# Attention with a fixed order on TensorE: a step's value products in pieces behind the next step's scores

## The chip, the cores and the metric

The kernel runs on one core of one Trainium2 chip. A time is device microseconds (us) of one execution; of several, the median is taken. The engines of the core are TensorE (PE; its weight loads are a row of their own, PEld), VectorE (DVE), ScalarE (ACT), GpSimd (POOL) and SyncE (SP), whose queue issues most of the DMAs. Each engine works through its own list of instructions in the order in which they stand there and waits on semaphores for the others.

## The reference

Two transformer blocks over 1024 tokens of width 1024. Two of its layers hold an attention over eight heads of width 64, and these are all that the change touches:

```
s = (einsum('bqhd,bkhd->bhqk', q_nope, k_nope) + einsum('bqhr,bkr->bhqk', q_rope, k_rope)) * scale
s = where(causal, s, -inf);  p = softmax(s);  o = einsum('bhqk,bkhd->bqhd', p, v)      # first layer
...
s = where(valid, q.k * HEAD_DIM**-0.5 - slope * distance, -inf)                        # mixing layer,
p = exp(s - max); o = p.v / sum(p); the branches are merged by their denominators      # three dilations
```

The kernel computes the three dilated branches as one causal attention with a table added to the scores, so both layers use one function. All matmuls are in 32-bit floats; products that need the precision are taken as a high and a low part.

## The kernel before, in words

The kernel is written against a layer that traces all instructions first and then fixes each engine's list with a scheduler: an instruction may stand anywhere that its data, the buffers of its pools and explicit edges allow. `turn(K, trace)` traces a piece of work so that its TensorE instructions stand behind the last TensorE instruction traced so far; in the attention of the kernel before nothing is held by it.

`attention` (L359) does one head. It takes the queries in four steps j = 0..3 of two blocks of 128 (u = 0, 1). In a step, for each block, the scores against keys 0..kend (kend = 128, 256, ... 1024) go to a bank of PSUM, in three matmul passes in the first layer and two in the mixing layer (L381). VectorE adds the mask or table and takes the row minimum (L385), ScalarE takes the exponential and the row sum (L387). Then, for each pair of key blocks, a *chunk*: three or four transposes (L394) turn the probabilities, ScalarE copies them from PSUM as the high part (`split`, L140), VectorE subtracts to get the low part (L141), and four products with the values (L400: high and low for each of two key blocks) add to the step's output. A step has j + 1 chunks. It closes with a copy on ScalarE (L403) and an add on VectorE (L404); after steps 1 and 3 the reciprocal sums are transposed (L410) and multiplied in (L412).

Around each head stands one `step(hd)` of the output projection (`early`, L725; matmuls L695): 12 matmuls of 512 columns in the first layer, 24 in the mixing layer, with rows of the layer's other half (`s`, loaded by SP at L708 and split on ScalarE and VectorE at L140 and L141). Its result is added to the residual on VectorE (L594) in the first layer and copied by ScalarE (L1793) in the mixing layer. SP also loads the query and key rows of a coming head (L608 and L610: eight DMAs in the first layer; L1810: six in the mixing layer) into one of two tiles, once the last scores of the head two before it have been read; behind them in SP's queue comes the load of `s`.

In the two attentions the scheduler interleaves scores, transposes, products and the projection of neighbouring steps and heads, and lets the products lag behind the scores. Pools: two PSUM tiles for scores and projection (`pa`), four for transposes and outputs (`pb`).

Of the kernel before, what the change touches and what calls it, by code (L numbers as in the profile page):

```python
# [14 lines left out]
AF = mybir.ActivationFunctionType  # L15
ALU = mybir.AluOpType
AX = mybir.AxisListType

P = 128
# [31 lines left out]
def _pools(ctx, tc):  # L51
    K = Ctx()
    K.tc = tc
    K.nc = tc.nc
    E = mybir.EngineType
    K.pe, K.sp, K.act, K.dve, K.pool = E.PE, E.SP, E.Activation, E.DVE, E.Pool
    mk = lambda n, b, **kw: ctx.enter_context(tc.tile_pool(name=n, bufs=b, **kw))
    K.cp = mk("cst", 1)
    K.px = mk("px", 4)
    K.pp = mk("pp", 4)  # L60
    K.pq = mk("pq", 4)
    K.pr = mk("pr", 2)
    K.ps = mk("ps", 2)
    K.pl = mk("pl", 3)
    K.pwst = mk("pwst", 2)
    K.pwh = mk("pwh", 4)
    K.pwl = mk("pwl", 4)
    K.pj = mk("pj", 1)
    K.pt = mk("pt", 2)
    K.pA = mk("psA", 2, space=bass.MemoryType.PSUM)  # L70
    K.pB = mk("psB", 4, space=bass.MemoryType.PSUM)
    K.pd = mk("dr", 1, space=bass.MemoryType.DRAM)
    K.n = 0
    K.last = None

    def nm(p):
        K.n += 1
        return f"{p}{K.n}"

    K.nm = nm  # L80
    K.X = lambda dt=F32R: K.px.tile([P, 4, 1024], dt, tag="x", name=nm("x"))
    K.P2 = lambda dt=F32: K.pp.tile([P, 2, 1024], dt, tag="p", name=nm("p"))
    K.Q2 = lambda dt=F32: K.pq.tile([P, 2, 1024], dt, tag="q", name=nm("q"))
    K.R2 = lambda dt=F32: K.pr.tile([P, 2, 1024], dt, tag="r", name=nm("r"))
    K.S = lambda dt=F32: K.ps.tile([P, 1024], dt, tag="s", name=nm("s"))
    K.L = lambda dt=F32: K.pl.tile([P, 1024], dt, tag="l", name=nm("l"))
    K.A = lambda: K.pA.tile([P, 1024], F32, tag="a", name=nm("pa"))
    K.B = lambda: K.pB.tile([P, 512], F32, tag="b", name=nm("pb"))
    K.junk = lambda: K.pj.tile([P, 512], mybir.dt.bfloat16, tag="j", name=nm("j"))
    K.DR = lambda shape, dt=F32: K.pd.tile(shape, dt, tag=nm("dt"), name=nm("d"))  # L90

    def small(cols, tag, dt=F32, bufs=2):
        return K.pt.tile([P, cols], dt, tag=tag, name=nm(tag), bufs=bufs)

    K.small = small
    return K
# [41 lines left out]
def split(K, hi, lo, src, eng=None):  # L138

    K.nc.scalar.activation(hi, src, AF.Copy)  # L140
    (eng or K.nc.vector).tensor_tensor(lo, src, hi.bitcast(F32), ALU.subtract)  # L141
# [26 lines left out]
def turn(K, trace):  # L168

    with K.tc.issue_after(anchor(K)):  # L170
        trace()
# [184 lines left out]
        nc.vector.scalar_tensor_tensor(out[:, s:], raw[:, :T - s], w(3 - s), out[:, s:], ALU.mult, ALU.add)  # L356


def attention(K, qb_passes, table, scale, vt, out, p0, ring, chunks):  # L359

    nc = K.nc
    st = K.small(24, "ast", bufs=3)
    low, tot, rec = (st[:, 8 * n:8 * n + 8] for n in range(3))
    for j in range(4):
        n = 2 * j + 2
        sm = []
        a = None  # L370
        for u in range(2):
            qb = 2 * j + u
            kend = (qb + 1) * P
            if j > 1 or u == 0:
                a = K.A()
            av = a if j > 1 else a[:, 512 * u:512 * u + 512]
            ps = qb_passes(qb)
            for h in range(0, kend, 512):
                e = min(kend, h + 512)
                for m, (lt, rt) in enumerate(ps):  # L380
                    nc.tensor.matmul(av[:, h:e], lt, rt[:, h:e], start=m == 0, stop=m == len(ps) - 1)  # L381
            s = ring(kend)
            sm.append(s)
            off = 896 - P * qb
            nc.vector.tensor_tensor_reduce(  # L385
                s, av[:, :kend], table[:, off:off + kend], -scale, 3.0e38, ALU.add, ALU.min, low[:, qb:qb + 1])
            nc.scalar.activation(s, s, AF.Exp, bias=low[:, qb:qb + 1], scale=-1.0, accum_out=tot[:, qb:qb + 1])  # L387
        o = K.B()
        for k0 in range(0, n, 2):
            blocks = [(k, u) for k in (k0, k0 + 1) for u in range(2) if k <= 2 * j + u]  # L390
            w = len(blocks) * P
            b = K.B()
            for c, (k, u) in enumerate(blocks):
                nc.tensor.transpose(b[:, c * P:(c + 1) * P], sm[u][:, k * P:(k + 1) * P], K.ident)  # L394
            ph, pl = chunks()
            split(K, ph[:, :w], pl[:, :w], b[:, :w])
            for k in (k0, k0 + 1):
                c0, c1 = (256 * (k - k0), min(256 * (k - k0) + 256, w))
                for m, pp in enumerate((ph, pl)):
                    nc.tensor.matmul(o[:, 256 - (c1 - c0):256], vt(k), pp[:, c0:c1],  # L400
                                     start=k == 0 and m == 0, stop=k == n - 1 and m == 1)
        oj = out[:, 256 * j:256 * j + 256]
        nc.scalar.activation(oj, o[64:128, 0:256], AF.Copy)  # L403
        nc.vector.tensor_tensor(oj, o[0:64, 0:256], oj, ALU.add)  # L404
        if j % 2:
            h = j // 2
            nc.vector.reciprocal(rec[:, 4 * h:4 * h + 4], tot[:, 4 * h:4 * h + 4])
            b = K.B()
            for q in range(4):
                nc.tensor.transpose(b[:, q * P:(q + 1) * P], rec[:, 4 * h + q:4 * h + q + 1].to_broadcast([P, P]), K.ident)  # L410
            oh = out[:, 512 * h:512 * h + 512]
            nc.vector.tensor_tensor(oh, oh, b[p0:p0 + 64], ALU.mult)  # L412


def layer_a(K, I, XT, get):
    nc = K.nc
# [18 lines left out]
    ydram = K.DR([8, P, T])  # L435
    gdram = [K.DR([P, T]) for _ in range(4)]
# [5 lines left out]
    for k in range(NK):  # L442
        for a, w in zip(heads, first):
            for h in (0, 512):
                for m, (l, r) in enumerate(((w[0], "h"), (w[0], "l"), (w[1], "h"))):
                    nc.tensor.matmul(a[:, h:h + 512], l[:, k, :], get(r, k)[:, h:h + 512],
                                     start=k == 0 and m == 0, stop=k == NK - 1 and m == 2)
# [105 lines left out]
    mask = K.L()  # L553
# [21 lines left out]
    vt = [K.R2(F32R), K.R2(F32R), K.Q2(F32R), K.Q2(F32R)]  # L575
# [3 lines left out]
    for ti in range(NT):  # L579
        o = K.B()  # L580
# [5 lines left out]
    ring, chunks = Ring(K, 2), Chunks(K)  # L586
# [12 lines left out]
    for p in range(4):  # L599
        yp = K.Q2()  # L600
        for u in range(2):
            hd = 2 * p + u
            K.heads.append(anchor(K))
            st = K.X()
            for z in range(2):
                for n in range(2):
                    d = st[:, 2 * z + n, :].bitcast(F32)
                    nc.sync.dma_start(d[0:64], qk_d[p][n][z][64 * u:64 * u + 64, :])  # L608
                    rs = qr_d[hd // 4][z][32 * (hd % 4):32 * (hd % 4) + 32, :] if n == 0 else kr_d[z][0:32, :]
                    nc.sync.dma_start(d[64:96], rs)  # L610
            Qh, Kh, Ql, Kl = (st[0:96, j, :] for j in range(4))

            def passes(qb):
                q = slice(qb * P, (qb + 1) * P)
                return [(Qh[:, q], Kh), (Qh[:, q], Kl), (Ql[:, q], Kh)]

            attention(K, passes, mask, 96 ** -0.5, lambda k: V(k)[:, hd, :], yp[64 * u:64 * u + 64, 0, :], 64 * u, ring, chunks)
            step(hd)
        nc.sync.dma_start(yp[:, 1, :], gdram[p])
        nc.vector.tensor_tensor(yp[:, 0, :], yp[:, 0, :], yp[:, 1, :], ALU.mult)  # L620
        nc.sync.dma_start(ydram[4 + p], yp[:, 0, :])
    K.tail = yp[:, 0, :]
    return ydram, zd

# [1095 lines left out]
def mix_layer(K, I, get, ydram):  # L1720
    nc = K.nc
# [76 lines left out]
    for p in range(4):  # L1798
        yp = K.R2()
        for u in range(2):  # L1800
            st = K.X()
            K.heads.append(anchor(K))
            tb = K.L()
            with deferred(K, K.heads[-2] if len(K.heads) > 1 else K.heads[-1]):
                nc.sync.dma_start(tb, I["dil"][2 * p + u])
            r = slice(64 * u, 64 * u + 64)
            with deferred(K, K.heads[-2] if len(K.heads) > 1 else None):
                for n, (m, o) in enumerate(((p, 0), (4 + p, 0), (4 + p, 1))):
                    for z in range(2):
                        nc.sync.dma_start(st[64 * z:64 * z + 64, n, :].bitcast(F32), qk_d[m][z ^ o][r, :])  # L1810
            if len(K.heads) == 1:
                nc.vector.tensor_copy(ring.t[1][:, 0, 0:8], sh[:, 0, 0:8].bitcast(F32))

            def passes(qb):
                q = st[:, 0, qb * P:(qb + 1) * P]
                return [(q, st[:, 1, :]), (q, st[:, 2, :])]

            hd = 2 * p + u
            attention(K, passes, tb, 0.125, lambda k: V(k)[:, hd, :], yp[64 * u:64 * u + 64, 0, :], 64 * u, ring, chunks)
            step(hd)  # L1820
        nc.sync.dma_start(ydram[p], yp[:, 0, :])
    K.tail = yp[:, 0, :]
    return zd

# [194 lines left out]
```

## Time and profile before

| | |
|---|---|
| time, median of 3 runs (lowest, highest) | 3291.51 us (3287.15, 3292.08) |
| the profiled execution, its own time | 3285.83 us |
| its span, mean granted TensorE clock | 3284.1 us, 0.971 |
| PE, DVE, ACT, POOL busy, share of the span | 94%, 67%, 49%, 24% |
| attention of the first layer, about | 258 to 456 us of the span |
| attention of the mixing layer, about | 2346 to 2541 us of the span |

A row of the timeline gives the start in us, the time in us, the engine, the line, the operation, what it writes and reads, how many were merged, and in brackets the idle time of that engine before it and what ended it. The time of a matmul is modelled to the moment its result is there, while the next one may start earlier; what one costs in a row of its like is read from start to start.

### The profile page before, as it was taken

What the parts mean: (1) busy time and instruction counts of PE and PEld (TensorE: products, weight loads), DVE (VectorE), ACT (ScalarE), POOL (GpSimd) and SP (SyncE); (2) the same over time, 40 slices, a digit from 0 to 9 for tenths busy, and PEclk for the clock granted to TensorE, in tenths of its full rate; (3) what the DMA queues carried; (4) which work ended last, traced back from release to release, by engine and by line L of the source; (5) the groups of instructions that cost most, each with busy time, mean ns of one, the idle gap of its engine ahead of it and who ended that gap; (6) DMA issues with size and microseconds to landing.
All of it is one profiled execution on the core that took longest, in us unless ns stands there. A gap on an engine that the chain in (4) does not pass through costs nothing. (4 is left out here: it accounts for less than half of the span.)

```text
span 3284.1 us, 42186 instructions
## 1 busy us (share of the span) xinstructions
PE 3077.9 (94%) x15560; PEld 2568.7 (78%) x15560; DVE 2211.5 (67%) x3637; ACT 1625.5 (49%) x2945; POOL 778.3 (24%) x487
## 2 busy tenths in 40 slices
PE   8999889999999989789999899899999799999998
PEld 6887777888897878578778777788787688888776
DVE  6537777356757556887775789736666955555997
ACT  5526543445555522655555443642565755554442
POOL 0000001113222221522233534100000432332543
PEclk9998999999999999899999999999999899999999
DMA  4157442334344565323332620354564322224223
GB/s 130 55 182 231 123 132 86 88 83 124 83 117 92 170 176 162 99 97 116 109 123 77 225 84 33 128 179 174 152 169 140 131 84 90 77 84 152 105 84 116
DMA packets 349567, 398.98 MB, mean 121 GB/s; under 512 B 21168, under 2 KB 279344, under 8 KB 349360
## 3 DMA queue, kind: packets, MB, share of 16 engines
q1 hardware_dynamic: 324016, 379.50, 37.1%
q10 hardware_dynamic: 25344, 16.78, 1.6%
q8 instruction: 123, 2.02, 0.3%
q14 instruction: 84, 0.69, 0.1%
HBM read 279.29 MB, written 116.92 MB: 121 GB/s over the span
## 5 line engine op out<-in xcount | busy, mean ns | idle before, releaser
L141 DVE TENSOR_TENSOR wlo<-wst,whi 128x1024 fp32r<-128x1024 f32 (+1 forms) x190 | 232.1, 1224 | 355.6 <-ACT whi L140 337.5
L185 PE MATMUL pa<-x,whi 128*128 128x512 f32 x1568 | 429.2, 395 | 1.8 <-DVE l L141 0.8
L140 ACT ACTIVATE whi<-wst 128x1024 fp32r<-128x1024 f32 (+1 forms) x190 | 180.1, 948 | 345.5 <-PE pa L185 86.0
L147 ACT ACTIVATE wst<-wst,pk 128x128 f32<-128x128 f32 (+1 forms) x816 | 251.7, 391 | 187.9 <-DMA wst<-in_ffn_w_in_dram 120.7
L185 PEld LDWEIGHTS pa<-x,whi 128*128 128x128 f32 x1568 | 292.0, 189 | 64.1 <-DVE x L141 1.8
L185 PE MATMUL pa<-x,wlo 128*128 128x512 f32 x784 | 244.2, 392 | 4.0 <-DVE wlo L141 4.0
L1325 PE MATMUL pa<-x,whi 128*128 128x512 f32 (+1 forms) x736 | 221.7, 384 | 4.2 <-ACT p L679 2.0
L1325 PE MATMUL pb<-x,whi 128*128 128x512 f32 (+1 forms) x736 | 224.0, 381 | 0.3 <-DVE r L141 0.3
L1404 PE MATMUL pa<-wlo,whi 128*128 128x512 f32 x768 | 188.5, 403 | 14.6 <-DVE wlo L141 12.7
L1404 PE MATMUL pb<-wlo,whi 128*128 128x512 f32 x744 | 182.2, 403 | 14.2 <-DVE wlo L141 14.2
L1288 POOL TENSOR_TENSOR s<-wst 128x512 f32<-128x512 f32 x44 | 57.9, 1317 | 561.2 <-ACT wst L147 525.4
L1404 PEld LDWEIGHTS pa<-wlo,whi 128*128 128x128 f32 x768 | 148.4, 194 | 52.3 <-DVE wlo L141 18.4
L1404 PEld LDWEIGHTS pb<-wlo,whi 128*128 128x128 f32 x744 | 143.9, 195 | 48.5 <-DVE wlo L141 18.2
L185 PEld LDWEIGHTS pa<-x,wlo 128*128 128x128 f32 x784 | 147.0, 188 | 38.8 <-DVE wlo L141 7.4
L937 POOL TENSOR_TENSOR s<-s,p 128x1024 f32<-128x1024 f32 x32 | 65.6, 2051 | 440.7 <-DMA s<-d 324.5
L1325 PEld LDWEIGHTS pa<-x,whi 128*128 128x128 f32 x736 | 136.8, 190 | 32.0 <-issue 2.6
L1325 PEld LDWEIGHTS pb<-x,whi 128*128 128x128 f32 x736 | 135.9, 188 | 26.9 <-DVE r L141 0.5
L140 ACT ACTIVATE whi<-s 128x1024 fp32r<-128x1024 f32 x88 | 93.0, 1057 | 117.5 <-POOL s L1289 67.1
L891 PE MATMUL pa<-whi,x 128*128 128x256 f32 x512 | 147.9, 289 | 0.0
L892 PE MATMUL pa<-wlo,x 128*128 128x256 f32 x512 | 145.1, 283 | 1.9 <-DVE wlo L141 1.9
L893 PE MATMUL pa<-whi,x 128*128 128x256 f32 x512 | 144.8, 283 | 0.0
L681 POOL TENSOR_TENSOR p<-p,q 128x1024 f32<-128x1024 f32 x8 | 21.1, 2641 | 515.0 <-DVE p L680 476.4
(591 smaller groups left out, 8056.9 us busy)
## 6 DMA issues: line engine op xcount, KB each, us to landing
wst<-in_ffn_w_in_dram SPq DMA_DIRECT2D x88, 512.0 KB, 3.8
d<-p SPq DMA_DIRECT2D x82, 512.0 KB, 3.5
d<-l SPq DMA_DIRECT2D x67, 512.0 KB, 3.9
x<-d SPq DMA_DIRECT2D x128, 256.0 KB, 5.4
p<-d SPq DMA_DIRECT2D x46, 512.0 KB, 4.7
wst<-in_s_w_in_dram SPq DMA_DIRECT2D x40, 512.0 KB, 4.0
s<-d SPq DMA_DIRECT2D x32, 512.0 KB, 9.6
l<-d SPq DMA_DIRECT2D x24, 512.0 KB, 5.6
```

The source lines that it names most:

```text
L140: K.nc.scalar.activation(hi, src, AF.Copy)
L141: (eng or K.nc.vector).tensor_tensor(lo, src, hi.bitcast(F32), ALU.subtract)
L147: K.nc.scalar.activation(st[:, k, :], st[:, k, :], AF.Copy, scale=col(K, gain, k0 + k))
L185: K.nc.tensor.matmul(ps[:, h:h + 512], w, x[:, h:h + 512], start=k == 0 and m == 0, stop=k == n - 1 and m == 2)
L681: nc.gpsimd.tensor_tensor(z, z, b, ALU.add)
L891: nc.tensor.matmul(o, xh, wh, start=k == 0, stop=False)
L892: nc.tensor.matmul(o, xh, wl, start=False, stop=False)
L893: nc.tensor.matmul(o, xl, wh, start=False, stop=k == NK - 1)
L937: nc.gpsimd.tensor_tensor(mv, mv, per_head(csT, P), ALU.subtract)
L1288: G(s1, a21, a22, ALU.add)
L1325: nc.tensor.matmul(p, l[:, k, :], r[:, k, :], start=k + m == 0, stop=k == 3 and m == 2)
L1404: nc.tensor.matmul(bank[j], th[:, a + o:a + o + P], tw[:, b:b + 512], start=c + m == 0, stop=c == n - 1 and m == 2)
```

## The change

`attention` is cut into functions: `scores` (one block), `flip` (transposes and split of a chunk), `product` (its four products) and `close`. A step's values become a list of pieces, K.pend, in the order flip 0, flip 1, product 0, flip 2, product 1, ..., close. Each step traces its first scores, then half of the pending pieces of the step before (which may belong to the head before), then its second scores, then the remaining pieces. Scores, pieces and `step(hd)` are each held by `turn`, so that TensorE's order in the two attentions is the order of the trace. What was done after a pair of heads (gate, store) becomes `fin`, part of the last `close`; `flush(K)` empties the list at the end of a layer. No instruction is added or taken away.

```
-def attention(K, qb_passes, table, scale, vt, out, p0, ring, chunks):
+def flush(K, keep=0):
+    while len(K.pend) > keep:
+        turn(K, K.pend.pop(0))
+
+def attention(K, qb_passes, table, scale, vt, out, p0, ring, chunks, fin=None):
...
+    def scores(j, u, a, sm):
...
+    def values(j, sm):
...
+        def flip(k0):
+            if k0 == 0:
+                parts["o"] = K.B()
...
+        def product(k0):
...
+        def close():
...
+            if j == 3 and fin is not None:
+                fin()
+        pieces = []
+        for k0 in range(0, n + 2, 2):
+            if k0 < n:
+                pieces.append(lambda k0=k0: flip(k0))
+            if k0:
+                pieces.append(lambda k0=k0: product(k0 - 2))
+        return pieces + [close]
+
+    for j in range(4):
+        sm = []
+        for u in range(2):
+            if j > 1 or u == 0:
+                a = K.A()
+            turn(K, lambda: scores(j, u, a, sm))
+            flush(K, 0 if u else len(K.pend) // 2)
+        K.pend = values(j, sm)
...
-            attention(K, passes, mask, 96 ** -0.5, lambda k: V(k)[:, hd, :], yp[64 * u:64 * u + 64, 0, :], 64 * u, ring, chunks)
-            step(hd)
+            attention(K, passes, mask, 96 ** -0.5, lambda k, hd=hd: V(k)[:, hd, :], yp[64 * u:64 * u + 64, 0, :], 64 * u,
+                      ring, chunks, fin if u else None)
+            turn(K, lambda: step(hd))
+    flush(K)
```

In the changed file the scores are L384, the transposes L403, the products L413, the reciprocals' transposes L426, the projection L734; on ScalarE the exponential is L390 and the output's copy L419.

TensorE, first layer, from the end of a head's last step into the next head. In the kernel before: scores `pa<-x`, transposes `pb<-ident,x`, products `pb<-p,r` (or `q`), with `x` the queries and keys or the probabilities.

```order
L381 MATMUL pa_2763<-x_2753 128x128 x3
L400 MATMUL pb_2352<-p_1622,r_1508 128x256
L394 MATMUL pb_2364<-ident,x_1621 128x128 x3
L410 MATMUL pb_2377<-ident,ast_2316 128x128 x4
L400 MATMUL pb_2352<-p_1622,r_1508 128x256 x3
L394 MATMUL pb_2402<-ident,x_1620 128x128 x4
L400 MATMUL pb_2352<-p_1622,r_1509 128x256
L381 MATMUL pa_2787<-x_2753 128x384 x3
L381 MATMUL pa_2763<-x_2753 128x256 x3
L400 MATMUL pb_2352<-p_1622,r_1509 128x256
```

And in the changed kernel:

```order
L734 MATMUL pa_2239<-whi_1634,s_2233 128x512 x2
L384 MATMUL pa_2264<-x_2254 128x128 x3
L403 MATMUL pb_2271<-ident,x_1621 128x128 x4
L403 MATMUL pb_2278<-ident,x_1621 128x128 x4
L413 MATMUL pb_2270<-p_1623,r_1508 128x256 x4
L403 MATMUL pb_2289<-ident,x_1621 128x128 x4
L413 MATMUL pb_2270<-p_1624,r_1509 128x256 x4
L384 MATMUL pa_2264<-x_2254 128x256 x3
L403 MATMUL pb_2305<-ident,x_1621 128x128 x3
L413 MATMUL pb_2270<-p_1624,q_1510 128x256 x4
L413 MATMUL pb_2270<-p_1625,q_1511 128x256 x2
L413 MATMUL pb_2270<-p_1625,q_1511 128x128 x2
```

All four chunks of step 3 now stand between the first scores of the next head and the transposes of its reciprocals, the first product right behind two sets of transposes; before, single products stood apart, with scores and transposes of other steps between them.

TensorE, first layer, a little later, steps 0 and 1 of a head. Before:

```order
L400 MATMUL pb_2180<-p_1622,r_1509 128x256
L394 MATMUL pb_2234<-ident,x_1621 128x128 x4
L381 MATMUL pa_2608<-x_2532 128x512 x3
L381 MATMUL pa_2608<-x_2532 128x128 x3
L381 MATMUL pa_2566<-x_2532 128x512 x3
L400 MATMUL pb_2180<-p_1622,r_1509 128x256 x3
L400 MATMUL pb_2180<-p_1623,q_1510 128x256
L400 MATMUL pb_2233<-p_1623,r_1508 128x256
```

Changed:

```order
L384 MATMUL pa_2328<-x_2254 128x384 x3
L403 MATMUL pb_2335<-ident,x_1621 128x128 x3
L413 MATMUL pb_2334<-p_1625,r_1508 128x256 x2
L413 MATMUL pb_2334<-p_1625,r_1508 128x128 x2
L384 MATMUL pa_2328<-x_2254 128x512 x3
L384 MATMUL pa_2352<-x_2254 128x512 x3
L384 MATMUL pa_2352<-x_2254 128x128 x3
L403 MATMUL pb_2362<-ident,x_1621 128x128 x4
L403 MATMUL pb_2369<-ident,x_1621 128x128 x3
L413 MATMUL pb_2361<-p_1622,r_1508 128x256 x4
```

Before, nine score matmuls stand between the transposes of chunk `pb_2234` and its first product (the last row). Now the single chunk of step 0 has nothing between its three transposes and its products, and the first chunk of step 1 has three transposes between.

ScalarE, first layer, changed kernel, after the last exponential of a head: high parts `p<-pb` of that head's step 3, the first exponential `x` of the next head, the split `s<-s` of a coming projection.

```order
L390 ACTIVATE x_1620,ast_2263<-x_1620,ast_2263 128x1024
L140 ACTIVATE p_1624<-pb_2493 128x512
L140 ACTIVATE p_1625<-pb_2500 128x512
L390 ACTIVATE x_1620,ast_2485<-x_1620,ast_2485 128x128
L140 ACTIVATE s_2900<-s_2900 128x256
L140 ACTIVATE p_1625<-pb_2511 128x512
L140 ACTIVATE p_1622<-pb_2527 128x384
```

The split of `s` stands ahead of the third and fourth chunk of step 3.

## Rows read from the trace of the kernel before

**Rows 1.** Windows, the two attentions: span, us busy (count) per engine, clock, DMA.

```profile
258.00:456.00 198.00, 181.93 (x1116) 159.91 (x1116) 141.54 (x298) 115.08 (x257) 0.00 (x0) 0.96 0.53 154
2346.00:2541.00 195.00, 179.99 (x1103) 154.55 (x1104) 133.74 (x293) 125.40 (x273) 0.00 (x0) 0.98 0.54 156
```

**Rows 2.** The same windows, matmuls of L695 alone (PE, PEld).

```profile
258.00:456.00 198.00, 39.47 (x156) 28.13 (x156) 0.96 0.53 154
2346.00:2541.00 195.00, 61.42 (x241) 43.45 (x242) 0.98 0.54 156
```

**Rows 3.** Waits of PE, first layer: engine, line, waited for, us, times, longest.

```profile
PE pb L400 <- ACT p L140: 9.7, 12, 2.8
```

**Rows 4.** Timeline of PE in a stretch without waits, first layer.

```profile
303.03 0.52 PE L400 MATMUL pb<-p,r 128*128 128x256 f32 x3
303.39 0.60 PE L394 MATMUL pb<-ident,x 128*128 128x128 f32 x4
303.74 1.47 PE L381 MATMUL pa<-x 96*128 96x512 f32 x6
305.05 0.49 PE L394 MATMUL pb<-ident,x 128*128 128x128 f32 x3
305.30 1.61 PE L381 MATMUL pa<-x 96*128 96x512 f32 x6
306.74 0.28 PE L400 MATMUL pb<-p,r 128*128 128x256 f32 x1
```

**Rows 5.** Timeline of VectorE and ScalarE, first layer.

```profile
300.65 0.68 DVE L385 CUSTOM_DVE_ANT_0 x<-pa,l 128x512 f32<-128x512 f32 x1
...
301.61 0.72 ACT L387 ACTIVATE x<-x,ast 128x512 f32<-128x512 f32 x1
...
303.75 0.96 DVE L385 CUSTOM_DVE_ANT_0 x<-pa,l 128x768 f32<-128x768 f32 x1
...
304.74 0.69 DVE L412 TENSOR_TENSOR q<-q,pb 64x512 f32<-64x512 f32 x1
304.75 0.94 ACT L387 ACTIVATE x<-x,ast 128x768 f32<-128x768 f32 x1
...
305.68 0.47 ACT L140 ACTIVATE p<-pb 128x384 fp32r<-128x384 f32 x1
...
307.08 0.55 DVE L141 TENSOR_TENSOR p<-pb,p 128x384 fp32r<-128x384 f32 x1
```

**Rows 6.** Timeline of ScalarE, mixing layer: the copy of a projection.

```profile
2385.96 1.02 ACT L1793 ACTIVATE wst<-pa 128x1024 f32<-128x1024 f32 x1 [0.28 <-PE pa L695]
```

**Rows 7.** Timeline, first layer: one chunk from its transposes to its products.

```profile
443.43 0.60 PE L394 MATMUL pb<-ident,x 128*128 128x128 f32 x4
443.79 0.65 PE L400 MATMUL pb<-p,r 128*128 128x256 f32 x4
444.07 0.60 ACT L140 ACTIVATE p<-pb 128x512 fp32r<-128x512 f32 x1 [0.88 <-PE pb L394]
...
444.72 0.38 PE L400 MATMUL pb<-p,r 128*128 128x256 f32 x1 [0.28 <-ACT p L140]
...
445.45 0.63 PE L400 MATMUL pb<-p,r 128*128 128x256 f32 x3 [0.34 <-DVE p L141]
```

**Rows 8.** Timeline of SP and ScalarE, first layer: loads of a head, then `s`.

```profile
306.93 0.45 SPq L608 DMA_DIRECT2D x<-d  x1
...
311.49 0.38 SPq L708 DMA_DIRECT2D s<-d  x1
...
316.34 0.42 ACT L140 ACTIVATE s<-s 128x256 fp32r<-128x256 f32 x1 [2.87 <-DMA s<-d]
```

**Rows 9.** Waits of ScalarE, first layer.

```profile
ACT s L140 <- DMA s<-d: 22.6, 8, 3.9
```

**Rows 10.** Windows around a wait of TensorE and behind it, first layer.

```profile
376.00:382.00 6.00, 3.17 (x16) 2.93 (x14) 4.20 (x13) 3.39 (x8) 0.00 (x0) 0.73 0.80 251
382.00:388.00 6.00, 6.00 (x34) 5.74 (x33) 2.88 (x9) 3.44 (x10) 0.00 (x0) 0.70 0.01 4
```

More of the change, by code (lines that the diff above doesn't have):

```diff
@@ L73, in _pools @@
     K.n = 0
-    K.last = None
+    K.last, K.pend = None, []
     def nm(p):
@@ L366, in attention @@
     low, tot, rec = (st[:, 8 * n:8 * n + 8] for n in range(3))
-    for j in range(4):
-        n = 2 * j + 2
[L369 to L389, printed above, removed]
+    def scores(j, u, a, sm):
+        qb = 2 * j + u
+        kend = (qb + 1) * P
+        av = a if j > 1 else a[:, 512 * u:512 * u + 512]
+        ps = qb_passes(qb)
+        for h in range(0, kend, 512):
+            e = min(kend, h + 512)
+            for m, (lt, rt) in enumerate(ps):
+                nc.tensor.matmul(av[:, h:e], lt, rt[:, h:e], start=m == 0, stop=m == len(ps) - 1)
+        s = ring(kend)
+        sm.append(s)
+        off = 896 - P * qb
+        nc.vector.tensor_tensor_reduce(
+            s, av[:, :kend], table[:, off:off + kend], -scale, 3.0e38, ALU.add, ALU.min, low[:, qb:qb + 1])
+        nc.scalar.activation(s, s, AF.Exp, bias=low[:, qb:qb + 1], scale=-1.0, accum_out=tot[:, qb:qb + 1])
+    def values(j, sm):
+        n = 2 * j + 2
+        parts = {}
+        def flip(k0):
+            if k0 == 0:
+                parts["o"] = K.B()
             blocks = [(k, u) for k in (k0, k0 + 1) for u in range(2) if k <= 2 * j + u]
@@ L396, in attention @@
             split(K, ph[:, :w], pl[:, :w], b[:, :w])
+            parts[k0] = ph, pl, w
+        def product(k0):
+            o, (ph, pl, w) = parts["o"], parts[k0]
             for k in (k0, k0 + 1):
@@ L401, in attention @@
                                      start=k == 0 and m == 0, stop=k == n - 1 and m == 1)
[L402 to L412, printed above, removed]
+        def close():
+            o = parts["o"]
+            oj = out[:, 256 * j:256 * j + 256]
+            nc.scalar.activation(oj, o[64:128, 0:256], AF.Copy)
+            nc.vector.tensor_tensor(oj, o[0:64, 0:256], oj, ALU.add)
+            if j % 2:
+                h = j // 2
+                nc.vector.reciprocal(rec[:, 4 * h:4 * h + 4], tot[:, 4 * h:4 * h + 4])
+                b = K.B()
+                for q in range(4):
+                    nc.tensor.transpose(b[:, q * P:(q + 1) * P], rec[:, 4 * h + q:4 * h + q + 1].to_broadcast([P, P]), K.ident)
+                oh = out[:, 512 * h:512 * h + 512]
+                nc.vector.tensor_tensor(oh, oh, b[p0:p0 + 64], ALU.mult)
+            if j == 3 and fin is not None:
[15 more added lines that the diff above has]
+        K.pend = values(j, sm)
 def layer_a(K, I, XT, get):
@@ L615, in passes, with fin @@
                 return [(Qh[:, q], Kh), (Qh[:, q], Kl), (Ql[:, q], Kh)]
-            attention(K, passes, mask, 96 ** -0.5, lambda k: V(k)[:, hd, :], yp[64 * u:64 * u + 64, 0, :], 64 * u, ring, chunks)
-            step(hd)
-        nc.sync.dma_start(yp[:, 1, :], gdram[p])
-        nc.vector.tensor_tensor(yp[:, 0, :], yp[:, 0, :], yp[:, 1, :], ALU.mult)
-        nc.sync.dma_start(ydram[4 + p], yp[:, 0, :])
+            def fin(p=p, yp=yp):
+                nc.sync.dma_start(yp[:, 1, :], gdram[p])
+                nc.vector.tensor_tensor(yp[:, 0, :], yp[:, 0, :], yp[:, 1, :], ALU.mult)
+                nc.sync.dma_start(ydram[4 + p], yp[:, 0, :])
+            attention(K, passes, mask, 96 ** -0.5, lambda k, hd=hd: V(k)[:, hd, :], yp[64 * u:64 * u + 64, 0, :], 64 * u,
+                      ring, chunks, fin if u else None)
+            turn(K, lambda: step(hd))
+    flush(K)
     K.tail = yp[:, 0, :]
@@ L1818, in mix_layer @@
             hd = 2 * p + u
-            attention(K, passes, tb, 0.125, lambda k: V(k)[:, hd, :], yp[64 * u:64 * u + 64, 0, :], 64 * u, ring, chunks)
-            step(hd)
-        nc.sync.dma_start(ydram[p], yp[:, 0, :])
+            fin = lambda p=p, yp=yp: nc.sync.dma_start(ydram[p], yp[:, 0, :])
+            attention(K, passes, tb, 0.125, lambda k, hd=hd: V(k)[:, hd, :], yp[64 * u:64 * u + 64, 0, :], 64 * u,
+                      ring, chunks, fin if u else None)
+            turn(K, lambda: step(hd))
+    flush(K)
     K.tail = yp[:, 0, :]
```

## The prediction, made before the changed kernel ran

> **What bounds the kernel now.** I read the page first (which engine is busy, and the clock), then windows over the two attentions, then TensorE's waits there, then timelines of single steps and chunks. Outside the attentions no order changes, so only these 393 us can move. In them TensorE is busy for 181.93 of 198 us and 179.99 of 195 us, VectorE and ScalarE well below, and the clock is nearly full, 0.96 and 0.98 [rows 1]. TensorE bounds both stretches. By its modelled ends it idles 16.1 + 15.0 = 31 us, of which the wait of products for the high part is the largest piece: 9.7 us in 12 waits, for some 80 chunks [rows 3]. So nearly all chunks are hidden now: while ScalarE and VectorE split one, TensorE has other steps' work in between.
>
> A head takes 23 us now. The first window holds 156 projection matmuls and the second 241, where eight heads have 96 and 192 [rows 2]; the surplus belongs to the next stage, 60 and 49 matmuls at about 0.23: (198 - 13.7) / 8 and (195 - 11.2) / 8 are both 23.0.
>
> What TensorE must issue per head, start to start [rows 4]: a product 0.12 (0.36 for three), a transpose 0.09 (0.35 for four), a 512-wide score matmul 0.24 (1.44 for six), a 384-wide one 0.20 (1.31 less three at 0.24, by three). Carried down by column, scores against 128 to 1024 keys in three passes cost 0.33, 0.46, 0.59, 0.72, 1.05, 1.18, 1.31, 1.44: 7.1 a head; 36 transposes 3.2; 40 products, eight of them half wide, 4.3; two reciprocal sets 0.7; twelve 512-wide projection matmuls 2.9. That is 18.2 in the first layer, and with two passes of scores (4.7) and 24 projection matmuls (5.8) 18.7 in the mixing layer. Before thus loses some 4.5 us a head to waits, clock and what this estimate misses.
>
> **The change part by part.** Nothing is removed or added. What changes is what stands between a chunk's transposes and its products.
>
> A bare chunk, nothing between: its last three products start 2.02 us after its first transpose (443.43 to 445.45: transposes, 0.60 on ScalarE, the subtraction on VectorE) [rows 7]. TensorE has 0.36 of transposes and 0.12 of the first product to issue in that time, so it stands still for 1.54 less whatever lies between. For a chunk of three transposes, with 0.47 and 0.55 in place of the copy and subtraction [rows 5], I get about 1.23. The first product waits for the high part, the second for the low part; both are waits of an in-order engine, and behind them stand the next scores, on which the next softmax hangs.
>
> First layer, one head, in the changed order, walking through the three queues:
> - Step 0's single chunk has no cover: 1.23, and 0.48 since VectorE has the normalisation (0.69 [rows 5]) ahead of its subtraction: 1.7.
> - Step 1. Its first transposes need both its softmaxes. The second scores end; 0.28 handover, 0.68 on VectorE, 0.72 on ScalarE, 0.05 back make 1.73 [rows 5, 7]; the next step's first scores cover 1.05. Left 0.7, and 0.3 of queue: 1.0. Then the first chunk, covered by three transposes (0.26): 1.28 and 0.4 of queue, 1.7. Together 2.7.
> - Step 2. The softmax over 768 keys takes 0.28 + 0.96 + 0.94 + 0.05 = 2.23 [rows 5]; step 1's last products, a reciprocal set and 1.31 of scores cover all but 0.1. The first chunk is covered by four transposes: 1.54 - 0.36 = 1.2. Together 1.35.
> - Step 3, behind the projection: the first chunk 1.2 and 0.2 of queue. The third and fourth stand on ScalarE behind the split of `s` (the order of ScalarE shows it). The load of `s` is issued behind eight loads, 4.56 us after their first, and lands 4.85 us later [rows 8], 9.4 us after the last scores of the head two before have freed the tile. ScalarE already waits for it, 22.6 us in 8 waits, 2.87 in the row shown [rows 8, 9], at no cost, since no product hangs on it. Now two chunks do. TensorE reaches the third chunk some 7.2 us after those scores and its copy would end near 8; behind `s` it ends near 10.7. Left are 2.5, then 0.6 for its low part and 0.5 for the fourth chunk. Together 5.0.
>
> Sum 1.7 + 2.7 + 1.35 + 5.0 = 10.8, and a head of 18.2 + 10.8 = 29.0: 6.0 more, 48 us in eight.
>
> Mixing layer: the same chunks, with a third less scores as cover and a copy of 1.02 on ScalarE for the projection [rows 6] ahead of the first chunk of step 3. By the same walk step 0 gives 1.8, step 1 3.1 (1.5 + 1.6), step 2 1.8, step 3 4.2 (2.15 for the first chunk; six loads instead of eight bring `s` sooner, so 2.0 for the third). Sum 11.0, head 18.7 + 11.0 = 29.7: 6.7 more, 54 us in eight.
>
> Moved DMAs: the gate's load and the pair's store go into the last close, half a head later. Both use SP's queue; the store waits there for VectorE's product, which is done before the next scores free a tile, so no load behind it is due. I take 0; if the `s` loads are pushed back, the bound is one wait of 3.9 us [rows 9] in each of eight pairs, 31 us.
>
> The sum is 48 + 54 = 102 on the profiled execution, 3285.83, so 3388. The median of the runs is 5.7 us (0.2%) above that execution; I forecast **3388** and leave the difference in the range.
>
> By the modelled busy time before loses 31 us, by starts some 4.5 a head, 72 us; I price by starts, because what was hidden under a modelled end is lost once TensorE must stop: the product at 444.72 shows 0.28 of idling, while the last start before it, the fourth of the products from 443.79 at 0.12 each, lies 0.57 back, of which 0.45 are lost [rows 7]. The Trainium skill ("Trainium Kernel Development and Optimization", section "Performance Expectations") calls matmul busy time a bad metric, since matmuls are pipelined. By the busy share alone one would expect at most those 31 us to be open to the order; the rows side with the page.
>
> **The rivals.**
> 1. *Only the bare covers count.* The queues turn out empty and `s` lands in time: step 3 costs 2.0, step 0 1.25, step 1 2.0, step 2 1.5, 6.7 a head in the first layer and 7.5 in the mixing layer. Heads 24.9 and 26.2, (1.9 + 3.2) x 8 = 41: **3327**. For it: my queue terms (0.3 to 0.5 each) rest on the order of lists walked by hand, and the wait for `s` now ends at no one's cost [rows 9]. Against: the order of ScalarE with `s` ahead of two chunks. A half-way case, `s` in time but the queues as walked, saves 2.9 and 1.0 a head, 31 us: 3357, inside the main case.
> 2. *The clock falls as well.* A long wait of TensorE (2.83 of 6 us idle) was followed by full work at a granted clock of 0.70, 0.73 in the first window [rows 10]: 0.27 x 6 + 0.30 x 6 = 3.4 us of clock lost for one such wait. With one a head, at `s` in step 3, and TensorE at work for 0.62 of the time, that is 2.1 a head, 34 us: **3422**. Against: most new waits are about 1 us, shorter than the 2.8 before that drop [rows 3, 10], with work between. The Trainium skill ("TensorE: Matmul & The Clock Gate", section "HAM oscillation — how this bites in real kernels") describes kernels in which a pause after each burst of matmuls puts TensorE on the lower of its two clocks, 1.2 instead of 2.4 GHz, each time anew. By that rule every head would pay; the trace shows such a fall once behind a pause, not yet a recurring one.
> 3. *Faster, since the fixed order takes away the waits that the scheduler left.* The place is the product's wait for the high part [rows 3] and the smaller ones around it. If each chunk had a full cover of 1.54 us, all 31 us of modelled idling could go: **3255**. It decides in favour of the change from that cover on; the changed order gives the first chunk of a step 0 to 0.36, and only the inner ones near 0.9. What is needed is three times what stands there, which counts against it.
> 4. *Little change.* The 4.5 us a head that before loses unseen are themselves bare chunks, whose waits the new order only puts elsewhere: heads of 23 to 24, 3285 to 3300. Against: its listed waits are few [rows 3].
>
> **How the numbers follow.** Forecast as walked (3355 to 3415) 0.52; rival 1 0.17; rival 2 0.18; rival 3 0.07; rival 4 0.06. The range leaves out rival 3, most of rival 4 and the far end of rival 2, where the clock and the SP queue add up: 3305 to 3440. A change of 0.2%, 6.6 us, is about what a measurement of this kernel can tell. Faster by more than that 0.08, within it 0.04, slower 0.88.
>
> **What would show it.** Right: windows of 29.0 and 29.7 us a head; TensorE's wait for the high and for the low part the two largest, together over 100 us in the two attentions with several waits per head; ScalarE's wait for `s` followed at once by a product's wait of 2 us or more, in each head of the first layer; transposes of step 1 waiting about 1 us for the exponential. Rival 1: the same places with waits near 1 and none behind `s`. Rival 2: a granted clock below 0.9 in either window. Rival 3: product waits below 9.7 us in all. It would be wrong at the root if TensorE in before were held by something that the fixed order removes and that the modelled ends hide: then heads come out below 23 us although products wait.

## The result and the profile after

The changed kernel takes 3453.23 us (median of 4 runs, 3447.1 to 3457.21) where the kernel before takes 3291.51: 1.0501 times as long, 95% interval [1.0485, 1.0516]. The direction was forecast; the size was not. The range ended at 3440.

The profiled execution of after has a span of 3445.3 us, 161.2 more than before. Cut by starts, at the last product of the first layer (455.4 before, 531.6 after), at the first scores of the mixing layer (2345.3, 2424.0) and at the last projection matmul behind it (2580.7, 2736.4), 76.2 of them lie up to the end of the first layer, 77.0 in the mixing layer with its end, 5.5 behind that, and 2.5 between the two. The first layer was forecast at 48, the mixing layer at 54.

Windows over seven heads of each attention, from the start of one projection to that of the last, and between them a single head of the first layer (columns as in [rows 1]):

```profile
281.00:511.70 230.70, 187.67 (x927) 156.63 (x925) 121.97 (x258) 96.29 (x219) 0.00 (x0) 0.80 0.32 92
...
346.20:379.90 33.70, 27.94 (x133) 23.24 (x133) 16.73 (x37) 13.53 (x31) 0.00 (x0) 0.75 0.30 82
...
2451.30:2659.90 208.60, 162.02 (x925) 133.03 (x926) 108.80 (x245) 102.48 (x225) 0.00 (x0) 0.97 0.35 95
```

Inside a layer a head takes 230.7 / 7 = 33.0 us in the first layer (29.0 forecast) and 208.6 / 7 = 29.8 in the mixing layer (29.7 forecast). The third column from the right, the granted clock, tells the two layers apart: it is 0.80 in the first and 0.97 in the mixing layer, where both had 0.96 to 0.98 before [rows 1].

TensorE's waits over the whole span (columns as in [rows 3], which holds the first layer alone), of products for the high and the low part in the kernel before:

```profile
PE pb L400 <- ACT p L140: 15.1, 19, 2.8
PE pb L400 <- DVE p L141: 3.6, 12, 0.6
```

and in after:

```profile
PE pb L413 <- ACT p L140: 54.8, 71, 2.9
...
PE pb L413 <- DVE p L141: 28.7, 67, 1.1
PE pb L403 <- ACT x L390: 16.2, 15, 4.0
```

Products waited 15.1 us for the high part in 19 waits before, 54.8 in 71 now. In five of the eight heads of the first layer a product waits 2.3 to 2.9 us behind the split of `s`; in one of them TensorE saw it so:

```profile
346.15 0.68 PE L734 MATMUL pa<-whi,s 128*128 128x512 f32 x2
...
353.06 0.49 PE L403 MATMUL pb<-ident,x 128*128 128x128 f32 x3
356.03 0.53 PE L413 MATMUL pb<-p,q 128*128 128x256 f32 x1 [2.48 <-ACT p L140]
...
362.92 3.40 PE L384 MATMUL pa<-x 96*128 96x512 f32 x9
...
379.94 0.68 PE L734 MATMUL pa<-whi,s 128*128 128x512 f32 x2
```

and ScalarE in front of it:

```profile
355.08 0.42 ACT L140 ACTIVATE s<-s 128x256 fp32r<-128x256 f32 x1 [3.65 <-DMA s<-d]
355.40 0.96 ACT L140 ACTIVATE p<-pb 128x512 fp32r<-128x512 f32 x2
```

The reader is to see the chain: ScalarE stands 3.65 us at the split of `s`, the two chunk copies behind it start at 355.40, and the third chunk's products follow at 356.03 after 2.48 of idling. Behind that, nine score matmuls at 362.92 take 3.40 us; in experiment 1 the same nine take 1.88.

### The profile page after: what moved, and what is told of

It is laid out like the page before. It is cut to its first block, busy times and chain, and to the rows that moved or that the text cites. A ratio compares the mean times of both kernels' runs of the same rounds, so it can differ in the third digit from the quotient of the medians.

```text
span 3445.3 us, 42227 instructions
## 1 busy us (share of the span) xinstructions
PE 3148.5 (91%) x15560; PEld 2613.8 (76%) x15560; DVE 2220.8 (64%) x3637; ACT 1629.7 (47%) x2945; POOL 777.9 (23%) x487
## 5 line engine op out<-in xcount | busy, mean ns | idle before, releaser
L930 PE MATMUL pa<-whi,x 128*128 128x256 f32 x512 | 147.9, 289 | 0.0
L1364 PE MATMUL pa<-x,wlo 128*128 128x512 f32 (+1 forms) x368 | 142.0, 387 | 4.5 <-DVE wlo L141 4.5
```

The source lines that it names most:

```text
L930: nc.tensor.matmul(o, xh, wh, start=k == 0, stop=False)
L1364: nc.tensor.matmul(p, l[:, k, :], r[:, k, :], start=k + m == 0, stop=k == 3 and m == 2)
```

## The experiments

All are compared by their ratio to the kernel before on the same chip, since that kernel itself took 3281 to 3292 us from one comparison to the next. 0.001 of the ratio is 3.3 us.

**1. The split of `s` later.**

```
+            if (j, u) == (2, 0):
+                K.late = [anchor(K, K.act)]
...
-            yv = stream_rows(K, ydram, rows[0], i, n=n)
+            with behind(K, K.late):
+                yv = stream_rows(K, ydram, rows[0], i, n=n)
```

> The changed kernel with one edit: the split of s for a projection is put behind the exponential of step 2's first block of the same head, a head later than it stood, on ScalarE. Theory (one wait of TensorE on s per head costs itself and the clock behind it): in the first layer the wait of 2.5 to 2.9 us before the third chunk of step 3 goes, the clock there rises from 0.75-0.81 to above 0.95, and a head falls from 33.0 us to about 26.5, 50 us in eight heads; in the mixing layer 1 us a head, 8 us. Together about 3395 us. Rival (the clock falls from the many waits of about 1 us that every head keeps): the wait goes, the clock stays near 0.8, some 31 us in all, 3420 us.

Measured: 3400.53 us, 1.0373 [1.0356, 1.0391]; against 1.0501 that is 42 us less, where the theory had 58 and the rival 31: between the two. The window over the same seven heads of the first layer:

```profile
279.40:483.30 203.90, 168.95 (x927) 141.20 (x926) 122.54 (x259) 96.67 (x220) 0.00 (x0) 0.90 0.37 105
```

29.1 us a head, 3.8 less than in after. TensorE's busy time for the same 927 matmuls falls from 187.67 us to 168.95, which is 2.7 a head; that is the clock. Only the other 1.1 are waits: the one at `s` goes, and others behind it grow. One of its heads, and the nine score matmuls in it:

```profile
339.50:367.50 28.00, 23.18 (x134) 19.38 (x134) 16.81 (x37) 13.63 (x31) 0.00 (x0) 0.94 0.37 99
...
351.79 1.88 PE L384 MATMUL pa<-x 96*128 96x512 f32 x9
```

They take 1.88 us where after took 3.40. But the mean clock rises to 0.90 and no further, 0.83 to 0.94 in the seven heads, although no wait of TensorE in them is longer than 1.5 us: part of the fall came from the wait at `s`, part from the waits near 1 us that stay.

**2. Work that nobody needs in the wait.**

```
+    def idle():
+        b = K.B()
+        for n in range(24):
+            nc.tensor.transpose(b[:, n % 4 * P:(n % 4 + 1) * P], K.ident, K.ident)
...
+            if k0 == 6 and j == 3 and len(qb_passes(0)) == 3:
+                pieces.append(idle)
```

> The changed kernel with 24 transposes of the identity that nothing reads (some 2.2 us of TensorE) put into the first layer's wait at s, between the fourth chunk's transposes and the third chunk's products of step 3. Theory (about half of what the wait costs is the slow clock behind it): the products start no earlier, but the clock of the first layer rises from 0.80 to 0.90 or more, a head falls from 33.0 to about 29.5 us, some 26 us in eight: about 3425 us with 2 us more work a head. Rival (the clock falls from the waits near 1 us in steps 0 to 2): clock and time as in the changed kernel, 3453 us, or up to 15 us more.

The kernel beside it:

> The changed kernel itself, beside the kernel with the filled wait on the same chip, for the comparison: 1.050 times the kernel before, first layer's clock 0.80.

Measured: 3435.34 us, 1.0454 [1.0438, 1.047], and the changed kernel again 3450.36, 1.0495 [1.0478, 1.0513]: 15 us less with 24 transposes more in each head of the first layer. Windows of seven heads of the filled kernel, and two of its heads:

```profile
282.30:498.60 216.30, 181.41 (x1095) 154.27 (x1093) 121.55 (x258) 96.20 (x219) 0.00 (x0) 0.94 0.35 99
...
347.30:376.10 28.80, 24.47 (x160) 20.56 (x158) 16.79 (x37) 13.55 (x31) 0.00 (x0) 1.00 0.36 96
376.10:406.40 30.30, 25.78 (x158) 21.91 (x158) 17.93 (x38) 13.57 (x31) 0.00 (x0) 0.94 0.44 127
```

and of the changed kernel beside it:

```profile
282.10:513.30 231.20, 187.78 (x927) 156.01 (x926) 121.94 (x258) 96.30 (x219) 0.00 (x0) 0.81 0.32 92
```

The head at a clock of 1.00, in the filled kernel's timeline: the filler (`pb<-ident`), then steps 0 and 1 of the next head:

```profile
354.27 0.49 PE L408 MATMUL pb<-ident,x 128*128 128x128 f32 x3
354.61 2.78 PE L395 MATMUL pb<-ident 128*128 128x128 f32 x24
357.14 1.85 PE L418 MATMUL pb<-p,q 128*128 128x256 f32 x8
...
359.81 0.49 PE L408 MATMUL pb<-ident,x 128*128 128x128 f32 x3
360.95 0.38 PE L418 MATMUL pb<-p,r 128*128 128x256 f32 x1 [0.64 <-ACT p L140]
361.69 0.56 PE L418 MATMUL pb<-p,r 128*128 128x256 f32 x3 [0.36 <-DVE p L141]
...
363.81 0.29 PE L408 MATMUL pb<-ident,x 128*128 128x128 f32 x1
364.75 0.88 PE L408 MATMUL pb<-ident,x 128*128 128x128 f32 x6 [0.64 <-ACT x L390]
366.48 0.39 PE L418 MATMUL pb<-p,r 128*128 128x256 f32 x1 [0.85 <-ACT p L140]
367.20 0.61 PE L418 MATMUL pb<-p,r 128*128 128x256 f32 x3 [0.34 <-DVE p L141]
```

The products start 2.9 us behind the fourth chunk's transposes (354.27), in after 3.0 (353.06, 356.03): the filler takes the place of the wait. The granted clock rises from 0.81 to 0.94, and a head takes 30.9 instead of 33.0. The head at a clock of 1.00 takes 28.8 us, with the wait at `s` filled and every other wait of the order in it: the 29.0 of the forecast. So the lost clock costs 33.0 - 28.8 = 4.2 a head, some 2 of it from the wait at `s`. The expectation, 26 us, was too high: the clock still falls in all but one of the seven heads.

**3. The mixing layer's last projection ahead of the last head.**

```
+            if hd == 7:
+                turn(K, lambda: step(hd))
             attention(...)
-            turn(K, lambda: step(hd))
+            if hd < 7:
+                turn(K, lambda: step(hd))
```

> The changed kernel with one edit: in the mixing layer the last head's projection stands ahead of that head's attention instead of behind it. Theory (the tile that its result holds keeps back the loads of the next stage's weights, so that TensorE has nothing to put into the last waits): the four weight loads start some 25 us earlier, and 15 to 20 us go at the end of the layer, about 3435 us. Rival (the end of the layer waits on the last pair's own output and its store): within 5 us of the changed kernel, 3453 us.

Measured: 3431.41 us, 1.0461 [1.0445, 1.0476], 13 us less; the theory holds, its 15 to 20 were a little high. SP's loads of the next stage's weights, first in the kernel before (start, us, line, tile, how many):

```profile
2507.07 0.44 SPq L156 DMA_DIRECT2D wst<-in_w_mix_out_dram  x1
...
2513.01 6.30 SPq L156 DMA_DIRECT2D wst<-in_w_mix_out_dram  x3
```

then in after:

```profile
2666.13 0.44 SPq L156 DMA_DIRECT2D wst<-in_w_mix_out_dram  x1
...
2672.07 1.40 SPq L156 DMA_DIRECT2D wst<-in_w_mix_out_dram  x2
...
2678.99 0.33 SPq L156 DMA_DIRECT2D wst<-in_w_mix_out_dram  x1
```

and in this kernel:

```profile
2636.18 0.44 SPq L156 DMA_DIRECT2D wst<-in_w_mix_out_dram  x1
2642.79 7.44 SPq L156 DMA_DIRECT2D wst<-in_w_mix_out_dram  x3
```

In before the first of the four loads is issued 32 us ahead of the last products of the attention (2538.9), in after 10 us ahead of them (2675.8): `wst` has two tiles, and the projections' results lie in them until they are stored. So the next stage's matmuls, which filled TensorE's gaps up to the last product, come behind it, and TensorE waits there, once for 5.85 us (after's timeline):

```profile
2692.85 1.22 PE L734 MATMUL pa<-whi,s 128*128 128x512 f32 x2 [5.85 <-ACT s L140]
```

In this kernel that wait is gone.

**4. The new order of tracing, held by nothing** (`turn(K, x)` becomes `x()` for scores, pieces and projection).

> The changed kernel with scores, pieces and projections traced in the same new order but held by nothing. Theory (the holding costs, not the order of tracing): the scheduler places transposes, scores and products apart again, product waits fall back to some 10 to 15 us in all, and the time is 3291 us within 0.5%. Rival (the tracing in pieces, with the last step's values in the next head, itself leads to a worse order): 3320 us or more.

Measured: 3285.6 us, 1.0019 [1.0005, 1.0033]. TensorE's waits for the split parts come to 12.8 us over the whole span, where the kernel before has 15.1 + 3.6 = 18.7:

```profile
PE pb L413 <- ACT p L140: 8.1, 13, 1.7
...
PE pb L413 <- DVE p L141: 4.7, 13, 1.1
```

The tracing in pieces costs at most 0.3%. Holding TensorE to this order costs the 5%.

**5. The first layer alone** (held as in after; the mixing layer traced and scheduled as before).

> The new order held in the first layer alone, the mixing layer traced and scheduled as before. Theory (the two layers add up, 76 us in the first as its trace shows): about 3368 us, mixing attention as long as before. Rival (part of the loss of the second layer comes from the first, by loads and tiles that arrive late): 3385 us or more, with the stages between later by more than the 76 us.

Measured: 3362.21 us, 1.0245 [1.0227, 1.0264]: 81 us for the first layer, which by difference leaves 84 for the other. From the first scores of the mixing layer to the last projection matmul behind it, this kernel takes 237.2 us where the kernel before takes 235.4. The layers add up within a few us.

**6. Two transposes ahead of each product.**

```
-        for k0 in range(0, n + 2, 2):
+        for k0 in range(0, n + 4, 2):
...
-            if k0:
-                pieces.append(lambda k0=k0: product(k0 - 2))
+            if k0 > 2:
+                pieces.append(lambda k0=k0: product(k0 - 4))
```

> The changed kernel with one edit: two transposes ahead of each product instead of one (flip 0, flip 1, flip 2, product 0, flip 3, product 1, ...), all else held as it is. Theory (a product waits because 0.36 us or nothing stands between its transposes and itself): another 0.4 to 0.8 us of cover for each chunk of steps 2 and 3, less for steps 0 and 1, heads shorter by 3 to 4 us in the first layer and 2 in the mixing layer, some 45 us: about 3405 us. Rival (VectorE and ScalarE are the ones that can't keep up): the waits only move to later pieces, less than 15 us, 3440 us.

Measured: 3413.28 us, 1.0397 [1.0381, 1.0412], 34 us less: nearer the theory in the sum, but not by layer. Inside the first layer a head takes 32.0 us, only 1 less, with the clock still at 0.79; inside the mixing layer 28.0 instead of 29.8. The waits for the high part fall from 54.8 us to 44.8, in 49 instead of 71:

```profile
PE pb L413 <- ACT p L140: 44.8, 49, 3.8
...
PE pb L413 <- DVE p L141: 24.6, 64, 1.0
```

**7. Both edits, 1 and 6.**

> Two transposes ahead and the split of s put late, both edits together. Theory: the two add up and the clock stays up in the first layer, above 0.93; heads of some 23 and 27 us, 20 to 30 us of waits in the mixing layer and 15 at the ends of the layers left against the kernel before: about 3330 us. Rival (the clock is lost in any held order with waits near 1 us): 3360 us or more.

Measured: 3381.23 us, 1.0303 [1.0285, 1.032]: 65 us less than after, but 50 above the theory; the rival's bound holds. A head takes 27.3 us in the first layer, at a clock of 0.92, and 28.0 in the mixing layer. More transposes ahead help only chunks that have a next chunk; steps 0 and 1 have one and two, and their products stay bare.

**8. The pieces in a spread order.** Each layer is traced from one list with 32 entries a head, each held by `turn`: S scores, F transposes, P products, Q a quarter of the projection; the last number is the head, -1 the one before. From its start:

```
ORDER = [('F', 2, 2, -1), ('Q', 3, 4, -1), ('P', 2, 0, -1), ('F', 3, 0, -1), ('P', 2, 1, -1), ('S', 0, 0, 0),
 ('S', 0, 1, 0), ('P', 2, 2, -1), ('F', 3, 1, -1), ('S', 1, 0, 0), ('F', 3, 2, -1), ('P', 3, 0, -1),
 ('F', 3, 3, -1), ('S', 1, 1, 0), ('P', 3, 1, -1), ('S', 2, 0, 0), ('P', 3, 2, -1), ('F', 0, 0, 0),
 ('P', 3, 3, -1), ('S', 2, 1, 0), ('P', 0, 0, 0), ('F', 1, 0, 0), ('S', 3, 0, 0), ('Q', 0, 4, 0),
...
```

> The attentions held in another order of the same pieces: the projection in four parts, and a chunk's transposes and its product always with a part of the scores or the projection, or both another transpose and another product, between them; the split of s late. Theory (what a held order costs is the missing cover alone): hardly any product waits, heads of 19 to 20 us against 23 before, 45 to 55 us less than the kernel before and some 10 us given back at the ends of the layers: about 3245 us, faster than the kernel before. Rival (the 23 us of a head before are set by VectorE, with some 17 us of work a head, and by queues that no order of TensorE frees): 3285 to 3310 us.

Measured: 3270.14 us, 0.9961 [0.9946, 0.9976]: faster than the kernel before by 0.4%, and between the theory and the rival. Three things are changed at once here, the order, the projection in four parts and the late split. Its waits in the first layer's attention (scores are L397 here, products L426):

```profile
PE pa L397 <- DVE ast L401: 8.8, 10, 1.1
...
PE pb L426 <- DVE p L141: 0.3, 1, 0.3
PE pb L426 <- ACT p L140: 0.2, 1, 0.2
```

and a stretch of TensorE:

```profile
334.40 0.60 PE L416 MATMUL pb<-ident,x 128*128 128x128 f32 x4
334.75 0.72 PE L426 MATMUL pb<-p,r 128*128 128x256 f32 x4
335.31 0.45 PE L397 MATMUL pa<-x 96*128 96x128 f32 x3
336.69 0.62 PE L397 MATMUL pa<-x 96*128 96x256 f32 x3 [0.93 <-DVE ast L401]
337.15 0.57 PE L426 MATMUL pb<-p,q 128*128 128x256 f32 x4
```

Products hardly wait any more, and from one projection to the next a head takes 20.1 us in either layer. The 23 us of the kernel before are not measured so: they are whole layers, less the next stage's matmuls, by eight. The same for this kernel:

```profile
253.50:434.20 180.70, 171.37 (x1116) 154.19 (x1116) 140.63 (x299) 115.50 (x258) 0.00 (x0) 0.97 0.59 174
2322.60:2505.60 183.00, 168.88 (x1070) 150.03 (x1068) 130.87 (x289) 122.98 (x263) 0.00 (x0) 0.94 0.53 152
```

With 60 and 12 matmuls of the next stage (L754) in them, a head takes (180.7 - 13.7) / 8 = 20.9 and (183.0 - 2.7) / 8 = 22.5 us: 2.1 and 0.5 less than before, 21 us in all and not the theory's 45 to 55. At the last product of the mixing layer the kernel is 33.6 us ahead of the kernel before, some 25 without the 36 matmuls of the next stage that it has still to do, and 4.9 us of this lead it had before the first attention began. At the last projection matmul behind that layer 17.0 are left, and 12 at the end. The 8 between are one wait behind its last products, as in experiment 3:

```profile
2524.86 1.22 PE L754 MATMUL pa<-whi,s 128*128 128x512 f32 x2 [8.46 <-ACT s L140]
```

**9. The spread order with the mixing layer's last projection one head earlier.**

> The spread order, and the mixing layer's last projection one head earlier (all four parts behind the seventh head's). Theory (the layer's end loses its filler through the tile that the last projection's result holds): the next stage's weights load some 15 us earlier, the waits of 8.5 and 1.6 us behind the last products shrink, 10 to 15 us: about 3257 us where the kernel before takes 3282. Rival (the end waits for the last pair's store and the loads that follow it): 3268 us or more.

Measured: 3260.41 us, 0.9929 [0.9916, 0.9943], 10 us less than without it, at the low end of what was expected. The fastest of all, with the next one within its interval.

**10. Another spread order.**

> The same with another order of the pieces, in which the last part of the projection and a chunk of step 2 stand between the first and the second scores of the next head. Theory (in the spread order one wait a head is left, at the second scores of step 0, for the tile that VectorE reads, 15.5 us in all): that wait goes, another 0.5 us a head, about 3250 us. Rival (the wait for the tile only moves to the scores of step 1): the same as the spread order with the last projection early, within 4 us.

Measured: 3261.47 us, 0.9934 [0.9921, 0.9948]: the time is the rival's. The wait for the tile did not only move, though: over the whole span it falls from 15.6 us to 9.9, and what takes the 5.7 back was not followed. These two orders without bare chunks are as good as each other.

## Why the prediction was wrong, and where it was right

**Right: the waits.** The walk through the three queues gave 29.0 and 29.7 us a head; the head at full clock took 28.8 (experiment 2), the mixing layer's heads 29.8. That is not luck of the sum: read by starts in the rows of that head, with the issue prices of the walk, step 0 stands still for 0.9 + 0.6 = 1.5 us (1.7 forecast), step 1 for 0.85 + 1.2 + 0.6 = 2.65 (2.7), and the third chunk's products come 2.6 late (2.5, with `s` ahead of them). Rival 1 (bare covers only, 24.9 and 26.2 a head) fell with that, rival 3 (faster) with the product waits, rival 4 (heads of 23 to 24) with both. Two signs were put too high. The waits for the high and the low part come to 54.8 + 28.7 = 83.5 us and not to over 100, and the product's wait behind `s` shows in five heads of eight and not in each. A slip without weight: the mixing layer's four steps add up to 10.9 and not 11.0.

**Failed: the clock was a rival and not a term.** The forecast stood on full-clock durations and left the slow clock to rival 2, at 2.1 a head, worked out from a single fall behind a single wait [rows 10] and weighed against because most new waits are near 1 us. Its sign, a clock below 0.9 in either window, came. In the first layer the clock fell in every head: 0.80 on average, 0.75 in the worst heads, 4.2 us a head by experiment 2, (33.0 - 29.0) x 8 = 32 us in all. That this is close to the 34 of rival 2 is luck: it had 2.1 in each of sixteen heads, and eight paid twice that while the mixing layer kept 0.97. Two points of the argument were wrong. The fall goes on: in [rows 10] 3.4 us of clock are lost in 12 us, while a head of 33.7 us at 0.75 loses 0.25 x 33.7 = 8.4; with TensorE at work for 0.62 of the time, as the prediction takes it, that is 5.2, and this head is 33.7 - 28.8 = 4.9 longer than the one at full clock. And waits near 1 us matter after all: with the long wait gone (experiment 1) the clock stays at 0.90, with it filled (experiment 2) at 0.94.

The trace of the kernel before could have told the second point. The prediction says that it shows such a fall once behind a pause; it shows another at the start of the mixing layer's attention, where no listed wait is longer than 1.2 us (a row of TensorE, and a window around it):

```profile
2348.96 0.48 PE L394 MATMUL pb<-ident,x 128*128 128x128 f32 x1 [1.19 <-ACT x L387]
...
2348.00:2354.00 6.00, 5.03 (x17) 3.90 (x17) 4.82 (x10) 3.28 (x10) 0.00 (x0) 0.52 0.09 38
```

The Trainium skill ("TensorE: Matmul & The Clock Gate", section "A second HAM failure mode: psum-queue depth-cycling") tells of a kernel in which short idling between groups of matmuls comes often enough to make the clock go to and fro between its two levels. The traces agree: in experiment 1, with no wait over 1.5 us, the clock of a head lies between 0.83 and 0.94, and in after, with the long wait, between 0.75 and 0.89. Why the mixing layer, whose products wait as often (35 waits for the high part in either layer, the longest 1.2 us there and 2.9 here), stays at 0.97 wasn't settled: it lacks the long wait at `s` and has twice the projection without a pause in it, and no run took these apart.

**Failed: the ends of a layer.** The sum counted eight heads and nothing around them. The mixing layer costs (77.0 - 6.8 x 8) = 23 us more than its heads. At its end the last projection was held behind the last head, its result kept the tile that the next stage's weights needed, and the filler came too late (experiment 3, which wins 13 back). The prediction followed the pair's store and the gate's load, not the projection's result. The other 10 were not taken apart; one place is the layer's first head, where the transposes wait for the exponential (after's timeline):

```profile
2444.43 1.18 PE L403 MATMUL pb<-ident,x 128*128 128x128 f32 x7 [4.03 <-ACT x L390]
```

Together 32 + 23 = 55 of the 59 us between 102 forecast and 161 measured; the first layer's start and end gave 4 back, and 8 lie between the layers and behind the second, in stages that hold the same work, and were not followed.

**The moved stores and gate loads** were put at 0; nothing in the waits of after contradicts it, and no run tested it by itself.

**The cause of the whole**: not the cutting into pieces (experiment 4, 1.0019), but an order that is held while it leaves chunks bare. The same pieces held in an order with something between each chunk's transposes and products, with the late split, the projection in parts and the last one early, beat the kernel before by 0.7%; how much of that is the order alone, no run shows.

## What to carry to other kernels

In this kernel an order fixed by hand paid only where the waits that it creates had cover. List, for each pair of a producer and its consumer on the bounding engine, what stands between, in us, against the time of the way round through the other engines, and mind what else stands in those queues (a split that waits for a DMA). Price each new pause of TensorE twice, once as itself and once as the slower matmuls behind it, with the granted clock of the stretch as the check. Follow what a moved step holds, its tiles too, to the end of the stage and into the next one's loads.

## What the hardware showed that was not expected

24 transposes that nothing reads, put into a wait, made the kernel 15 us faster, 1.0454 against 1.0495 times the kernel before; the granted clock of the first layer was 0.94 with them and 0.81 without. In the same kernel a head at 1.00 and one at 0.94 differ by 1.5 us, 28.8 and 30.3. And the clock fell where the trace lists no wait of TensorE above 1.2 us (0.52 at the start of the mixing layer in the kernel before).
